# Another order of products and up blocks in the feed-forward stage of a two-layer decoder trunk

## The chip, the cores and the metric

The kernel runs on one core of a Trainium2 chip. The metric is the device time of one execution in microseconds (us): the median of several runs, on a chip that also gives one profiled execution with a trace of every engine. The engines that matter here are TensorE (PE in the rows; its weight loads are PEld), VectorE (DVE), ScalarE (ACT), GpSimd (POOL) and SyncE (SP), whose queue issues most transfers.

## The reference, cut to what matters

The program is two layers of a decoder on 256 tokens of width 2048, all in 32-bit floats. Each layer has a mixer (a projection, sliding-window attention, gated linear attention, an output projection) and a feed-forward stage. The change touches the feed-forward stage alone:

```
for l in range(2):
    ...                                          # mixer
    h = rmsnorm(x, norm2_g[l])                   # 256 x 2048
    u = jnp.square(jax.nn.relu(h @ w_up[l]))     # w_up:   2048 x 8192
    x = x + u @ w_down[l]                        # w_down: 8192 x 2048
```

## The kernel before, in words

**Exact products from two halves.** Every 512 x 512 block of a weight is loaded as f32 (1 MB), copied on ScalarE to a coarser form `wh` (L173, two instructions) and subtracted on VectorE to a rest `wl` (L174). TensorE then multiplies with both halves. A block may have its halves ready up to three blocks ahead of the one that TensorE works on, because `wh` and `wl` have three buffers (`WBUFS`): the halves of block i+3 can't be written before TensorE is done with block i. `prep` writes the halves, `fetch` issues the load. The raw weights of the up projection have two buffers.

**Up blocks.** `h @ w_up` is made 512 columns of the hidden width at a time, an index i from 0 to 15, each in four up blocks (kb 0 to 3) into four PSUM accumulators (`block_a`, L243 and L245: 16 matmuls of 512 columns and 16 of 256). After the last of the four, `up_done` moves the accumulators out (ScalarE L861, VectorE L862), and ScalarE applies relu and square (L863, L864). There are only four accumulators, so the next i waits for them.

**Chunks and products.** The hidden width is worked off in chunks c of 1024: chunk c is made of the up indices 2c and 2c+1. Its product with w_down is done for two column halves p = 0 and 1, in each with seven block products in place of eight (the Strassen-Winograd scheme), named 1, 2, 6, 5, 7, 3, 4 in the order in which they run. Each product is twelve matmuls of 512 columns (`block_p`, L257, L259, L261), after which VectorE adds the result to x (`add_to`, L892 or L894). The eighth chunk is done in the plain way, with 8 down blocks.

**The weight combinations.** A `Super` holds the four 512 x 512 quarters x, w, y, z of w_down for one chunk and half, each with one buffer. Product 1 uses x, 2 uses w. For product 6, VectorE makes x+y in place (L87) and t = that + z (L89). Two accumulating transfers on GpSimd's queue then make y+z in place (L92, for product 7) and t+w (L95, for product 4). Product 5 uses the new x, product 3 uses z. The loads of x and w are issued one block ahead of product 1's turn to be fetched, those of y and z at product 2's.

**The activation combinations.** `split` makes the two halves of a combination of the hidden activations (ScalarE L869, VectorE L870). `split_rest(c)` runs when the last up block of chunk c is done and makes six of the seven (12, s2, s1, s3, s4, 22, with four more VectorE operations, L879 to L885). Each has one buffer.

**Order.** `FFN_ORDER` starts with eight up blocks (i = 0 and 1). Then follow seven periods, one for each chunk c = 0 to 6: the 14 products of chunk c with the 8 up blocks of chunk c+1 put between them as the tuple `BETWEEN` says (0 is an up block). Written with U for an up block and the half as an index, a period before is

1a U 2a 6a U 5a 7a U 3a 4a U 1b 2b U 6b 5b U 7b 3b U 4b U

so that the last up block of chunk c+1 stands directly ahead of product 1 of chunk c+1. The instruction streams of the engines are fixed before the run by a planner, which takes the written order as priority and its own estimates of times, and so lets instructions of neighbouring blocks swap places. Each engine then goes through its stream in that order.

Of the kernel before, what the change touches and what calls it, by code (L numbers as in the profile page):

```python
# [17 lines left out]
P = 128  # L18
S = 256
NT = S // P  # L20
# [24 lines left out]
WBUFS = 3  # L45


BETWEEN = (1, 0, 2, 6, 0, 5, 7, 0, 3, 4, 0, 1, 2, 0, 6, 5, 0, 7, 3, 0, 4, 0)


@with_exitstack
def trunk(ctx, tc, x, norm1_g, w_in, q_norm_g, k_norm_g, attn_sinks, gla_gate_w,
# [9 lines left out]
    def bank(name):  # L62
        return misc.tile([P, 512], F32, tag="m", name=name)


    blocks, supers, forms = [], [], {}
    ff = [None]

    class Super:
# [14 lines left out]
        def form(self, prod):  # L84
            t = self.t
            if prod == 6:
                nc.vector.tensor_tensor(t["x"], t["x"], t["y"], ALU.add)  # L87
                t["t"] = ff[0].tile([P, 4, 512], F32, tag="qt", name=f"qt{self.name}")
                nc.vector.tensor_tensor(t["t"], t["x"], t["z"], ALU.add)  # L89
            if prod == 5:  # L90
                for a in range(0, 4, 2):
                    nc.gpsimd.dma_start(t["y"][:, a:a + 2], t["z"][:, a:a + 2],  # L92
                                        accum_op=ALU.add, max_dma_last_dim=2048)
                for a in range(0, 4, 2):
                    nc.gpsimd.dma_start(t["t"][:, a:a + 2], t["w"][:, a:a + 2],  # L95
                                        accum_op=ALU.add, max_dma_last_dim=2048)
            return t[{1: "x", 2: "w", 6: "t", 5: "x", 7: "y", 3: "z", 4: "t"}[prod]]

    def plan(layer):
        for cols in IN_CHUNKS:  # L100
            for kb in range(4):
                blocks.append((w_in[layer], kb * 512, cols))
        for n, kb in OUT_ORDER:
            blocks.append((w_out[layer], kb * 512, (n * 512, n * 512 + 512)))
        for u in FFN_ORDER:
            if u[0] == "up":
                _, i, kb = u
                blocks.append((w_up[layer], kb * 512, (i * 512, i * 512 + 512)))
            elif u[0] == "down":
                _, c, n, kb = u  # L110
                blocks.append((w_down[layer], c * 1024 + kb * 512, (n * 512, n * 512 + 512)))
            else:
                _, c, p, prod = u
                if prod == 1:
                    blocks.append(Super(w_down[layer], c * 1024, p * 1024, f"{layer}{c}{p}"))
                    supers.append((len(blocks) - 1, blocks[-1]))
                else:
                    blocks.append(supers[-1][1])
                forms[len(blocks) - 1] = prod

    IN_CHUNKS = [(1024, 1536), (0, 512), (512, 1024), (4360, 4624), (1536, 2048),
# [5 lines left out]
    FFN_ORDER = [("up", i, kb) for i in range(2) for kb in range(4)]  # L127
    for c in range(7):
        ups = [("up", i, kb) for i in (2 * c + 2, 2 * c + 3) for kb in range(4)]
        for k, step in enumerate(BETWEEN):  # L130
            if step == 0:
                FFN_ORDER.append(ups.pop(0))
            else:
                FFN_ORDER.append(("product", c, BETWEEN[:k].count(1) - (step != 1), step))
    FFN_ORDER += [("down", 7, n, kb) for n in range(4) for kb in range(2)]
    for l in range(DEPTH):
        plan(l)
# [97 lines left out]
    def block_a(accs, rhs, first, last, kts):  # L235

        i = next_block()
        wh, wl = halves.pop(i)
        for f in range(4):
            for k in range(4):  # L240
                a = rhs[kts[k]]
                fs = slice(f * P, (f + 1) * P)
                nc.tensor.matmul(accs[f], wh[:, k, fs], a,  # L243
                                 start=(first and k == 0), stop=False)
                nc.tensor.matmul(accs[f][:, :S], wl[:, k, fs], a[:, :S], start=False,  # L245
                                 stop=(last and k == 3))
            if f % 2:
                tick()
        prep_to(i + 1 + WBUFS)
# [600 lines left out]
    def feed_forward(l, norm2):  # L850
        fp = ff[0]
        hT2 = norm2.hT
        nxt = Norm(f"i{l + 1}", n1cols, (l + 1) * KT, False) if l + 1 < DEPTH else None
        ur, a = {}, {}

        def up_done(i, accs):

# [9 lines left out]
        def split(name, c, src):  # L867
            d = fp.tile([P, 4, 2, P], F32R, tag="as1" if name == "21" else f"a{name}", name=f"a{name}{l}{c}")
            nc.scalar.activation(d[:, :, 0], src, AF.Copy)  # L869
            nc.vector.tensor_tensor(d[:, :, 1], src, d[:, :, 0].bitcast(F32), ALU.subtract)  # L870
            a[name] = d

        def split_rest(c):

            a11, a21 = (ur[2 * c][:, :, T * P:(T + 1) * P] for T in range(NT))
            a12, a22 = (ur[2 * c + 1][:, :, T * P:(T + 1) * P] for T in range(NT))
            split("12", c, a12)
            s1 = fp.tile([P, 4, P], F32, tag="s1", name=f"s1{l}{c}")
            nc.vector.tensor_tensor(s1, a21, a22, ALU.subtract)  # L879
            nc.vector.tensor_tensor(a21, a11, a21, ALU.subtract)  # L880
            nc.vector.tensor_tensor(a11, s1, a11, ALU.subtract)
            split("s2", c, a11)
            split("s1", c, s1)
            split("s3", c, a21)
            nc.vector.tensor_tensor(a12, a11, a12, ALU.add)  # L885
            split("s4", c, a12)
            split("22", c, a22)

        def add_to(n, T, ps, sign=ALU.add):
            x, r = xs[T, n], norm2.r[:, T:T + 1]  # L890
# [6 lines left out]
        ps = {}  # L897
        for step in FFN_ORDER:
            if step[0] == "up":
                _, i, kb = step  # L900
                if kb == 0:
                    accs = [acc.tile([P, 512], F32, tag="a", name=f"up{l}{i}{f}")
                            for f in range(4)]
                block_a(accs, hT2, kb == 0, kb == 3, range(4 * kb, 4 * kb + 4))
                if kb == 3:
                    up_done(i, accs)
                    if nr is None:
                        nr = sm.tile([P, NT], F32, tag="nr", name=f"nr{l}")
                        nc.vector.tensor_scalar(nr, norm2.r, -1.0, None, ALU.mult)
                    if i == 0:  # L910
                        split("11", 0, ur[0][:, :, :P])
                    elif i == 15:
                        for j, k in enumerate("12"):
                            for T in range(NT):
                                split(f"{T + 1}{k}", 7,
                                      ur[14 + j][:, :, T * P:(T + 1) * P])
                    elif i % 2:
                        split_rest(i // 2)
            elif step[0] == "product":
                _, c, p, prod = step  # L920
                n1, n2 = 2 * p, 2 * p + 1
                if prod in (1, 2, 5):
                    ps[prod] = bank(f"dn{l}{c}{p}{prod}")
                o = ps[{1: 1, 6: 1, 7: 1, 4: 1, 2: 2, 5: 5, 3: 5}[prod]]
                block_p(o, a[{1: "11", 2: "12", 6: "s2", 5: "s1", 7: "s3", 3: "s4",
                              4: "22"}[prod]], prod in (1, 2, 5), True)
                if p == 1 and prod == 1 and c < 6:
                    split("11", c + 1, ur[2 * c + 2][:, :, :P])
                if prod == 1 or prod == 2:
                    add_to(n1, 0, o)  # L930
                elif prod == 6:
                    add_to(n2, 0, o, ALU.subtract)
                elif prod == 5:
                    add_to(n2, 1, o)
                elif prod == 7:
                    add_to(n2, 1, o, ALU.subtract)
                elif prod == 3:
                    add_to(n2, 0, o)
                else:
                    add_to(n1, 1, o)  # L940
            else:
                _, c, n, kb = step
                if kb == 0:
                    accs = [acc.tile([P, 512], F32, tag="a", name=f"dn{l}{c}{n}{T}")
                            for T in range(NT)]
                block_b(accs, [a["11"], a["21"]] if kb == 0 else [a["12"], a["22"]],
                        kb == 0, kb == 1, None)
                if kb == 0:
                    continue
                for T in range(NT):  # L950
                    add_to(n, T, accs[T])
                    if nxt is None:
                        nc.scalar.dma_start(
                            out[0, T * P:(T + 1) * P, n * 512:(n + 1) * 512], xs[T, n])
                if nxt is not None:
                    add(nxt.chunk(n), now[0] + 2)
# [49 lines left out]
```

## Time and profile before

| | us |
|---|---|
| median of 3 runs | 2107.3 (2105.09 to 2109.97) |
| the profiled execution | 2106.07 |
| its span, first to last instruction | 2104.1 |
| PE busy | 2039.3 (97%) |
| DVE busy | 1598.7 (76%) |
| ACT busy | 1225.6 (58%) |

The busy time of PE counts matmuls whose ends are modelled and which overlap, so a share of 97% still leaves room. What a matmul really takes is read from the distance between the starts of two that follow each other. The feed-forward stage of layer 0 lies between 368 and 1052 us. Its seven periods begin near 393 us, and they are some 89 us long.

### The profile page before, as it was taken

How to read it: one execution, taken by the hardware profiler on the slowest of the kernel's cores; microseconds unless marked ns; L12 is line 12 of the kernel's file. 1: busy time of each engine (PE TensorE's matmuls, PEld its weight loads, DVE VectorE, ACT ScalarE, POOL GpSimd, SP SyncE). 2: the span in 40 equal slices, each digit the busy share in tenths (PEclk: the TensorE clock that was granted, in tenths of full speed). 3: DMA queues.
4: the chain of work that ended last, by engine and by line, in shares of the span. 5: the costliest groups of instructions: out<-in, count | busy, mean ns of one | idle time of the engine just before them, and what ended most of it. 6: DMA issues, size and time to landing. Idle time of an engine off the chain costs nothing.

```text
span 2104.1 us, 26079 instructions
## 1 busy us (share of the span) xinstructions
PE 2039.3 (97%) x10238; PEld 1693.9 (81%) x10238; DVE 1598.7 (76%) x1442; ACT 1225.6 (58%) x1681; POOL 190.6 (9%) x198
## 2 busy tenths in 40 slices
PE   8999999999999999999999999999999999999999
PEld 7877888887777878778888878888877878778787
DVE  5676565888888888879656756658888888888884
ACT  5575554656665565656555755546665656666663
POOL 3200000001110001101002000000111001110000
PEclk9999999999999999999999999999999999999999
DMA  6544366787888878796555444578879787888864
GB/s 223 181 161 161 122 197 231 225 259 209 240 221 254 255 229 233 215 253 183 199 180 162 160 148 150 186 246 238 232 222 246 222 263 229 216 240 225 260 179 160
DMA packets 227707, 442.61 MB, mean 210 GB/s; under 512 B 8276, under 2 KB 16544, under 8 KB 227584
## 3 DMA queue, kind: packets, MB, share of 16 engines
q1 hardware_dynamic: 195472, 379.87, 52.3%
q0 software_dynamic: 30912, 58.97, 17.7%
q10 hardware_dynamic: 1200, 2.11, 0.3%
q8 instruction: 80, 1.31, 0.3%
q14 instruction: 43, 0.35, 0.0%
HBM read 380.10 MB, written 2.10 MB: 182 GB/s over the span
## 4 chain that ended last, share of the span: by engine, by line
PE 68%; DVE 14%; issue 8%; ACT 7%; DMA 3%; SPq 0%; ACTq 0%; DVEq 0%
PE up L243 14%; DVE wl L174 7%; PE up L245 7%; PE in L228 6%; PE in L227 6%; PE in L229 6%; ACT wh L173 5%; PE dn L259 4%; PE dn L261 4%; PE dn L257 4%; PE wo L228 3%; DVE qt L89 3%; PE wo L229 3%; PE wo L227 3%; DVE qx L87 2%
## 5 line engine op out<-in xcount | busy, mean ns | idle before, releaser
L174 DVE TENSOR_TENSOR wl<-raw,wh 128x2048 fp32r<-128x2048 f32 (+1 forms) x256 | 569.8, 2226 | 318.7 <-ACT wh L173 314.4
L243 PE MATMUL up<-hf,wh 128*128 128x512 f32 x2048 | 713.6, 398 | 23.7 <-ACT wh L173 12.3
L173 ACT ACTIVATE wh<-raw 128x1024 fp32r<-128x1024 f32 (+1 forms) x512 | 500.6, 1025 | 400.5 <-PE up L243 140.8
L245 PE MATMUL up<-hf,wl 128*128 128x256 f32 x2048 | 531.8, 282 | 4.2 <-DVE wl L174 4.2
L243 PEld LDWEIGHTS up<-hf,wh 128*128 128x128 f32 x2048 | 384.5, 189 | 106.3 <-ACT wh L173 16.2
L245 PEld LDWEIGHTS up<-hf,wl 128*128 128x128 f32 x2048 | 388.8, 190 | 29.2 <-DVE wl L174 10.5
L227 PE MATMUL in<-wh,hi 128*128 128x512 f32 (+1 forms) x640 | 237.9, 375 | 3.2 <-ACT hi L352 3.2
L228 PE MATMUL in<-wl,hi 128*128 128x512 f32 (+1 forms) x640 | 237.6, 373 | 0.0
L229 PE MATMUL in<-wh,hi 128*128 128x512 f32 (+1 forms) x640 | 235.1, 370 | 0.0
L257 PE MATMUL dn<-wh,as 128*128 128x512 f32 x448 | 174.1, 394 | 16.2 <-ACT as L869 16.2
L259 PE MATMUL dn<-wl,as 128*128 128x512 f32 x448 | 176.4, 394 | 3.6 <-DVE wl L174 3.4
L261 PE MATMUL dn<-wh,as 128*128 128x512 f32 x448 | 174.7, 390 | 0.0
L174 DVE TENSOR_TENSOR wl<-qx,wh 128x2048 fp32r<-128x2048 f32 x56 | 128.0, 2286 | 46.9 <-ACT wh L173 46.9
L173 ACT ACTIVATE wh<-qx 128x1024 fp32r<-128x1024 f32 x112 | 112.3, 1050 | 75.5 <-PE dn L261 39.7
L173 ACT ACTIVATE wh<-qt 128x1024 fp32r<-128x1024 f32 x112 | 112.5, 1053 | 71.3 <-DVE qt L89 36.4
L92 POOL DMA_DIRECT2D qy<-qz x56 | 68.1, 1448 | 898.5 <-DVE qx L87 821.4
L892 DVE SCALAR_TENSOR_TENSOR x<-dn,vf,x 128x512 f32<-128x512 f32 x156 | 116.0, 744 | 34.0 <-PE dn L261 19.1
L227 PEld LDWEIGHTS in<-wh,hi 128*128 128x128 f32 x640 | 120.1, 188 | 25.1 <-ACT hi L352 3.5
L228 PEld LDWEIGHTS in<-wl,hi 128*128 128x128 f32 x640 | 120.6, 188 | 22.1 <-issue 1.5
L229 PEld LDWEIGHTS in<-wh,hi 128*128 128x128 f32 x640 | 120.2, 188 | 20.1 <-issue 0.8
L257 PE MATMUL dn<-wh,a 128*128 128x512 f32 x336 | 132.5, 394 | 3.3 <-ACT a L869 3.3
L261 PE MATMUL dn<-wh,a 128*128 128x512 f32 x336 | 131.3, 391 | 0.6 <-DVE a L870 0.6
(202 smaller groups left out, 2957.7 us busy)
## 6 DMA issues: line engine op xcount, KB each, us to landing
raw<-in_w_up_dram SPq DMA_DIRECT2D x128, 1024.0 KB, 6.8
raw<-in_w_in_dram SPq DMA_DIRECT2D x63, 1024.0 KB, 5.1
raw<-in_w_out_dram SPq DMA_DIRECT2D x32, 1024.0 KB, 5.0
qx<-in_w_down_dram SPq DMA_DIRECT2D x28, 1024.0 KB, 8.4
qw<-in_w_down_dram SPq DMA_DIRECT2D x28, 1024.0 KB, 5.2
qy<-in_w_down_dram SPq DMA_DIRECT2D x28, 1024.0 KB, 9.3
qz<-in_w_down_dram SPq DMA_DIRECT2D x28, 1024.0 KB, 10.0
qy<-qz POOLq DMA_DIRECT2D x56, 512.0 KB, 6.6
```

Of the source, the lines that this page charges most:

```text
L92: nc.gpsimd.dma_start(t["y"][:, a:a + 2], t["z"][:, a:a + 2], accum_op=ALU.add, max_dma_last_dim=2048)
L173: nc.scalar.activation(wh[:, ks, :n], src[:, ks], AF.Copy)
L174: nc.vector.tensor_tensor(wl[:, :, :n], src, wh[:, :, :n].bitcast(F32), ALU.subtract)
L227: nc.tensor.matmul(o, ah, wh[:, k, :n], start=(first and k == 0), stop=False)
L228: nc.tensor.matmul(o, ah, wl[:, k, :n], start=False, stop=False)
L229: nc.tensor.matmul(o, al, wh[:, k, :n], start=False, stop=(last and k == 3))
L243: nc.tensor.matmul(accs[f], wh[:, k, fs], a, start=(first and k == 0), stop=False)
L245: nc.tensor.matmul(accs[f][:, :S], wl[:, k, fs], a[:, :S], start=False, stop=(last and k == 3))
L257: nc.tensor.matmul(o, ah, wh[:, k], start=(first and k == 0), stop=False, skip_group_check=not first)
L259: nc.tensor.matmul(o, ah, wl[:, k], start=False, stop=False, skip_group_check=not first)
L261: nc.tensor.matmul(o, al, wh[:, k], start=False, stop=(last and k == 3), skip_group_check=not first)
L892: nc.vector.scalar_tensor_tensor(x, ps, r, x, ALU.mult, ALU.add)
```

## The change

`BETWEEN` has the same 14 products and 8 up blocks in another order. A number of 10 or more is half b, one of 20 or more belongs to the next chunk. With a dash for the next chunk, the period is now

U U 2a U U 6a 5a U 7a 3a U 4a 1b U 2b 6b 5b U 7b 3b 1a' 4b

and product 1a of chunk 0 is put ahead of the first period. In the last period 1a' falls away. So the last up block of a chunk is followed by four products, three of which belong to the old chunk and one is the next chunk's first, and two up blocks stand ahead of product 2.

Three things follow in the code. The combinations s3, s4 and 22 of the next chunk can't be written while products 7b, 3b and 4b of the old one still read theirs, so `split_rest` leaves them in `late`, and each is made right after its product (in chunk 0 at once). The combinations of the eighth chunk are made after the last product in place of after the last up block. And a `Super` is looked up by its chunk and half, since two are alive at once. Apart from that, the accumulating transfer y+z is issued with product 6 and no longer with product 5.

```diff
-BETWEEN = (1, 0, 2, 6, 0, 5, 7, 0, 3, 4, 0, 1, 2, 0, 6, 5, 0, 7, 3, 0, 4, 0)
+BETWEEN = (0, 0, 2, 0, 0, 6, 5, 0, 7, 3, 0, 4, 11, 0, 12, 16, 15, 0, 17, 13, 21, 14)
...
-            if prod == 5:
                 for a in range(0, 4, 2):
                     nc.gpsimd.dma_start(t["y"][:, a:a + 2], t["z"][:, a:a + 2],
                                         accum_op=ALU.add, max_dma_last_dim=2048)
+            if prod == 5:
...
                 if prod == 1:
-                    blocks.append(Super(w_down[layer], c * 1024, p * 1024, f"{layer}{c}{p}"))
-                    supers.append((len(blocks) - 1, blocks[-1]))
-                else:
-                    blocks.append(supers[-1][1])
+                    supers[layer, c, p] = Super(w_down[layer], c * 1024, p * 1024,
+                                                f"{layer}{c}{p}")
+                blocks.append(supers[layer, c, p])
...
-        for k, step in enumerate(BETWEEN):
+        if c == 0:
+            FFN_ORDER.append(("product", 0, 0, 1))
+        for step in BETWEEN:
             if step == 0:
                 FFN_ORDER.append(ups.pop(0))
-            else:
-                FFN_ORDER.append(("product", c, BETWEEN[:k].count(1) - (step != 1), step))
+            elif step < 20 or c < 6:
+                FFN_ORDER.append(("product", c + step // 20, step // 10 % 2, step % 10))
...
             split("s1", c, s1)
-            split("s3", c, a21)
             nc.vector.tensor_tensor(a12, a11, a12, ALU.add)
-            split("s4", c, a12)
-            split("22", c, a22)
+            late[7], late[3], late[4] = ("s3", c, a21), ("s4", c, a12), ("22", c, a22)
...
-                    elif i == 15:
-                        for j, k in enumerate("12"):
-                            for T in range(NT):
-                                split(f"{T + 1}{k}", 7,
-                                      ur[14 + j][:, :, T * P:(T + 1) * P])
-                    elif i % 2:
+                    elif i % 2 and i < 15:
                         split_rest(i // 2)
+                        if i == 1:
+                            for prod in (7, 3, 4):
+                                split(*late.pop(prod))
...
+                if p == 1 and prod in late:
+                    split(*late.pop(prod))
+                if (c, p, prod) == (6, 1, 4):
+                    for j, k in enumerate("12"):
+                        for T in range(NT):
+                            split(f"{T + 1}{k}", 7, ur[14 + j][:, :, T * P:(T + 1) * P])
```

## Rows read from the trace of the kernel before

**Rows 1.** Window of one whole period: length, busy time of each engine, PEclk, DMA share, GB/s.

```profile
573.00:661.80 88.80, 84.77 (x424) 70.48 (x424) 76.78 (x61) 54.53 (x63) 9.64 (x8) 1.00 0.83 237
```

**Rows 2.** Timeline of PE, an undisturbed up block and product: start us, us, instruction.

```profile
641.62 1.07 PE L243 MATMUL up<-hf,wh 128*128 128x512 f32 x4
...
647.24 0.40 PE L257 MATMUL dn<-wh,a 128*128 128x512 f32 x1
...
649.99 0.84 PE L243 MATMUL up<-hf,wh 128*128 128x512 f32 x3
```

**Rows 3.** Timeline of PE where two chunks meet; in brackets idle time and releaser.

```profile
566.88 0.40 PE L257 MATMUL dn<-wh,a 128*128 128x512 f32 x1
...
572.32 0.28 PE L245 MATMUL up<-hf,wl 128*128 128x256 f32 x1
573.54 0.47 PE L243 MATMUL up<-hf,wh 128*128 128x512 f32 x1 [0.94 <-DVE ur L862]
...
576.27 0.28 PE L245 MATMUL up<-hf,wl 128*128 128x256 f32 x1
577.58 1.20 PE L243 MATMUL up<-hf,wh 128*128 128x512 f32 x4 [1.03 <-ACT wh L173]
579.05 0.50 PE L257 MATMUL dn<-wh,a 128*128 128x512 f32 x1 [0.27 <-ACT a L869]
...
581.13 0.50 PE L257 MATMUL dn<-wh,as 128*128 128x512 f32 x1 [1.35 <-ACT as L869]
```

**Rows 4.** Waits of PE over the whole span: us in total, times, longest us.

```profile
PE dn L257 <- ACT as L869: 16.2, 12, 1.4
PE up L245 <- DVE wl L174: 4.2, 14, 0.3
```

**Rows 5.** Timeline of DVE at the same meeting of two chunks.

```profile
570.78 2.28 DVE L174 TENSOR_TENSOR wl<-qw,wh 128x2048 fp32r<-128x2048 f32 x1
572.98 0.41 DVE L862 TENSOR_TENSOR ur<-up,us 128x256 f32<-128x256 f32 x1
573.31 0.74 DVE L892 SCALAR_TENSOR_TENSOR x<-dn,vf,x 128x512 f32<-128x512 f32 x1
...
574.30 2.28 DVE L174 TENSOR_TENSOR wl<-qt,wh 128x2048 fp32r<-128x2048 f32 x1
576.60 0.69 DVE L879 TENSOR_TENSOR s<-ur,ur 128x512 f32<-128x512 f32 x1
...
580.86 1.28 DVE L870 TENSOR_TENSOR a<-ur,a 128x512 fp32r<-128x512 f32 x2
```

**Rows 6.** Timeline of ACT: a copy that waited for TensorE, one that waited for a load.

```profile
562.11 2.01 ACT L173 ACTIVATE wh<-raw 128x1024 fp32r<-128x1024 f32 x2 [1.50 <-DMA raw<-in_w_up_dram]
...
647.33 2.01 ACT L173 ACTIVATE wh<-qx 128x1024 fp32r<-128x1024 f32 x2 [3.49 <-PE up L243]
```

**Rows 7.** Timeline of PE, the end of a product 1b.

```profile
616.19 0.39 PE L257 MATMUL dn<-wh,a 128*128 128x512 f32 x1
```

**Rows 8.** Timeline of POOL, the transfers t+w of the same half.

```profile
623.59 2.41 POOL L95 DMA_DIRECT2D qt<-qw  x2 [8.14 <-DVE wl L174]
```

**Rows 9.** Timeline of SP's queue, the reload of that half's tiles.

```profile
626.17 0.37 SPq L80 DMA_DIRECT2D qx<-in_w_down_dram  x1
633.40 0.37 SPq L80 DMA_DIRECT2D qw<-in_w_down_dram  x1
```

**Rows 10.** DMA issues over the whole span: KB each, median us to landing.

```profile
raw<-in_w_up_dram SPq DMA_DIRECT2D x128, 1024.0 KB, 6.8
...
qz<-in_w_down_dram SPq DMA_DIRECT2D x28, 1024.0 KB, 10.0
```

**Rows 11.** Window with the densest transfers, columns as in the first group.

```profile
639.00:650.00 11.00, 11.00 (x58) 9.33 (x57) 7.93 (x6) 6.04 (x6) 0.00 (x0) 1.00 1.05 386
```

**Rows 12.** Longest wait of POOL's queue over the whole span.

```profile
POOL qy L92 <- DVE qx L87: 821.4, 26, 35.6
```

**Rows 13.** Timeline of PE at the first down block of layer 0.

```profile
1013.69 0.50 PE L227 MATMUL dn<-wh,a 128*128 128x512 f32 x1 [0.35 <-DVE ur L862]
```

More of the change, by code (lines that the diff above doesn't have):

```diff
@@ L63, in bank @@
         return misc.tile([P, 512], F32, tag="m", name=name)
-    blocks, supers, forms = [], [], {}
+    blocks, supers, forms = [], {}, {}
     ff = [None]
@@ L853, in feed_forward @@
         nxt = Norm(f"i{l + 1}", n1cols, (l + 1) * KT, False) if l + 1 < DEPTH else None
-        ur, a = {}, {}
+        ur, a, late = {}, {}, {}
         def up_done(i, accs):
@@ L922, in feed_forward @@
                 if prod in (1, 2, 5):
-                    ps[prod] = bank(f"dn{l}{c}{p}{prod}")
-                o = ps[{1: 1, 6: 1, 7: 1, 4: 1, 2: 2, 5: 5, 3: 5}[prod]]
+                    ps[c, p, prod] = bank(f"dn{l}{c}{p}{prod}")
+                o = ps[c, p, {1: 1, 6: 1, 7: 1, 4: 1, 2: 2, 5: 5, 3: 5}[prod]]
                 block_p(o, a[{1: "11", 2: "12", 6: "s2", 5: "s1", 7: "s3", 3: "s4",
```

## The prediction

> **What bounds the kernel now.** I read the window of one period of the feed-forward stage first. It is 88.8 us long; PE counts as busy for 84.8, DVE for 76.8, ACT for 54.5, and the DMA engines for 83% [rows 1]. There the reader is to see that TensorE is close to full, but not full, with VectorE next. How much is missing is read from undisturbed blocks: an up block takes 647.24 - 641.62 = 5.62 us, a product 649.99 - 647.24 = 2.75 us [rows 2]. Eight up blocks and 14 products make 8 x 5.62 + 14 x 2.75 = 83.5 us. So TensorE loses 88.8 - 83.5 = 5.3 us in a period, 14 x 5.3 = 74 us in the program. The granted clock was full in that window, so there is no more in it than these waits.
>
> Next comes PE's timeline where two chunks meet. From the distances of starts, less 0.12 us for a short matmul and 0.23 for a long one (2.75 / 12; 5.62 / 16 - 0.23), four waits stand in 15 us [rows 3]:
> - 572.32 to 573.54: 1.10 us, for VectorE to empty an accumulator;
> - 576.27 to 577.58: 1.19 us, for ScalarE's `wh`;
> - 577.58 to 579.05, four matmuls: 0.55 us, for the combination 12 of product 2a;
> - 579.05 to 581.13, two matmuls: 1.62 us, for s2 of product 6a.
>
> Together 4.46 us. The list of PE's waits shows the wait for `as` 12 times and never longer than 1.4 us, one for each of the 6 meetings in a layer, so the same happens at every meeting. That is 12 x 4.46 = 53.5 us. The other 0.9 us of a period are waits for `wl` in the blocks after the two formations of x+y and t; such a wait stands in the list 14 times at `up` alone [rows 4].
>
> Why they come: DVE runs there without a pause. It makes `wl` of 2a, empties accumulators, adds, makes `wl` of 6a and only then the combinations [rows 5]. Combination 12 is used 579.05 - 566.88 = 12.2 us after the last up block, s2 after 14.3. The written order gives them 2.75 + 5.62 = 8.4 and 11.1 us.
>
> **The change, part by part.** No block, matmul or VectorE operation is added or removed; all terms are waits.
>
> *The meeting.* After the last up block now come four products, 4 x 2.75 = 11.0 us, then two up blocks, then 2a. The next up block needs its accumulators after 11.0 us; the third was emptied at 573.4, 6.5 us after the last up block's end, the fourth behind one more addition, some 1.1 later. Combination 12 is needed after 11.0 + 2 x 5.62 = 22.2 us, and took 12.2. s2 is needed after 22.2 + 2.75 + 11.2 = 36.2, and took 14.3. Three of the four waits thus lose their cause with 4 us or more to spare. The wait for `wh` came from ScalarE having relu, square and a copy in one line; that can return in another place, and I price it as new.
>
> *The run of four products*, which is what is late next. Halves of block i+3 can start when block i is done: `wh` 2.0 us [rows 6], `wl` 2.2 (start to start, 570.78 to 572.98), and two products are 5.5 us, so 1.3 us are spare. Per product DVE also has an addition, 0.7, and in three of the four a late split, 0.6 [rows 5]: 3.5 us against 2.75. It falls back 3 x 0.75 + 0.15 = 2.4 us. Less the spare 1.3, and the 0.9 us that four `wh` matmuls can run ahead of `wl` [rows 2], 0.2 us of wait remain. From above: all 4.7 us of `split_rest`'s other work (four operations of 0.7, three splits of 0.64) fall among these four too. I take 0.8 a meeting, towards the 1.19 that a misplaced `wh` costs now: 12 x 0.8 = 9.6 us. Both ends stay in the range.
>
> *Formations.* Ahead of 6a now stand two up blocks more, so its wait goes: half of 0.9, 14 x 0.44 = 6 us. 6b is still two blocks (an up block and 2b) behind 1b, and its wait stays. If 6a's stays too, the sum is 6 worse.
>
> *Start and end of the stage.* Chunk 0 makes all its combinations at once, but 2a follows 14.0 us later instead of 8.4; nothing. The eighth chunk's four splits are written after the last product; the first down block waits 0.35 us now, 0.5 with its restart [rows 13]. If the planner leaves them there it waits a copy and a subtraction, 1.25; if it pulls them up, 0. I take 0.5 more per layer, 1 us; bounds -1 and +4 (all eight pieces).
>
> *y+z with product 6.* GpSimd's queue stood idle 821 us in 26 waits for x+y itself [rows 12]. It already issues as soon as x+y is there, whichever product it is written with: 0, on both sides.
>
> *Loads.* Each load keeps its place beside its block, but on SP's queue the x and w of the next 1a are now followed at once by two up loads. That is a rival below.
>
> Sum, against the profiled execution: 2106.1 - 53.5 + 9.6 - 6 + 1 = 2057; its span is 2104.1, the rest lies around it. The median of the runs is 1.2 above it, so 2058 us.
>
> **Rivals.**
>
> *The loads come late.* The reload of w waits for the transfer t+w: it was issued 633.40 - 616.19 = 17.2 us after product 1b had ended [rows 7, 9], 9.8 after the transfer's issue [rows 8]. In the new order 30.5 us lie between 1b's end and the period's first up block (5.62 + 8.25 + 5.62 + 11.0), whose load stands behind w. The densest window moved 386 GB/s [rows 11], 2.7 us for one load. So that load lands near 17.2 + 0.5 + 2.7 + 6.8 [rows 10] = 27.2, its halves are ready at 31.4, and 30.5 to 31.4 is when they are used: on the edge. With the 10.0 us that z needs it would be 3.2 later, some 2 us of wait beyond my 0.8: 12 x 2 = 24, 2082 us. For it: ScalarE already waits for up loads, 1.5 us in one case [rows 6]. Against: before product 1a' SP has little else to do.
>
> The Trainium skill ("DMA: Bandwidth & Descriptors", Specifications) gives a core about 358 GB/s from HBM. The window's 386 is above it; by the page a load would take 2.9 us and the estimate would move by 0.4 us, against the change.
>
> *VectorE in strict written order: slower.* If the stream has `split_rest` ahead of the halves of 4b, then from the last up block's end: halves of 1a' 4.2, accumulators 0.7, relu and square 2.1 (as two copies of the same size), `split_rest` 4.7, `wl` of 4b 2.2: 13.9 us. It is needed after 3 x 2.75 + 0.23 = 8.5. Every meeting then waits 5.4 in place of 4.46: 2106.1 + 12 x 0.95 - 6 + 1 = 2113. It decides once `wl` of 4b is ready over 13.4 us after that up block. For it: the accumulators at 572.98 stood behind `wl` of 2a. Against: `wl` of 6a ran at 574.30, ahead of `s` at 576.60, though it is written after it [rows 5].
>
> The Trainium skill ("TensorE: Matmul & The Clock Gate", Architectural detail) calls the queues of ScalarE and VectorE strict first-in, first-out. By that rule what the planner wrote can't be mended by the engine, and this rival stands or falls with the stream; the trace agrees in so far as DVE worked through its list while TensorE waited 1.10 us for 0.4 us of work.
>
> *Nothing: VectorE is the bound.* It is busy for 76.8 us of a period and idle for 12.0 now; my 2058 asks that it idle about 8. If its waits for `wh` (ScalarE idles up to 3.5 us for a buffer [rows 6]) are only moved, the period stays 88.8: 2103 to 2110.
>
> **How the numbers follow.** The forecast, 2042 to 2072, has 0.53. Nearly no new wait, under 2042 (all 74 us would be 2032): 0.09. Late loads or orders like it, 2072 to 2102: 0.20. Nothing: 0.05. The slower rival: 0.13. A difference of 0.2%, 4 us, can be told from none. So faster 0.82, the same 0.05, slower 0.13. The range 2036 to 2095 leaves out the last two and a little at both ends.
>
> **What would show it.** Right: periods of 84 to 85.5 us; no wait of PE for `as`, `a` or `ur` at the meetings; the wait for `wl` ahead of 6a gone, that of 6b still there; PE's waits at 3b, 1a', 4b and the first up block under 1.5 us in sum; GpSimd's wait for x+y as long as now. Wrong: ACT idle for an up load over 2 us at each meeting (loads), PE waiting over 4 us for `wl` at 4b (written order), or DVE idling 12 us in a period of 88.

## The result and the profile after

| | before, us | after, us |
|---|---|---|
| median | 2106.72 (2105.09 to 2109.97) | 2070.51 (2068.42 to 2071.34, 4 runs) |
| the profiled execution | 2106.07 | 2071.34 |
| its span | 2104.1 | 2069.6 |

The ratio is 0.9825, 95% interval 0.9808 to 0.9842: 36.2 us faster, where 49 were forecast. In the changed kernel lines shift by two: `wh` is L175, `wl` L176, the up block L245 and L247, the product L259 to L263, x+y L88, t L90, y+z L92.

First the page after: the busy time of each engine, and the engines' shares of the chain that ended last (the chain of work followed back from the last instruction).

```profile
PE 2028.8 (98%) x10238; PEld 1699.8 (82%) x10238; DVE 1598.6 (77%) x1442; ACT 1222.4 (59%) x1681; POOL 190.5 (9%) x198
...
PE 78%; DMA 11%; DVE 6%; issue 4%; ACT 1%; SPq 0%; POOL 0%; DVEq 0%; ACTq 0%; POOLq 0%
```

The same row of the chain before:

```profile
PE 68%; DVE 14%; issue 8%; ACT 7%; DMA 3%; SPq 0%; ACTq 0%; DVEq 0%
```

The work is the same and DVE is no busier; VectorE and ScalarE have left most of the chain, and transfers have a larger share of it, 11% in place of 3%. Now TensorE's waits over the whole span (us in all, times, longest), of which [rows 4] has the old ones.

```profile
PE up L247 <- DVE wl L176: 15.3, 15, 3.8
...
PE dn L261 <- DVE wl L176: 0.2, 1, 0.2
```

No line for `as`, `a` or `ur` is left. TensorE's line for `wl` in an up block has grown from 4.2 to 15.3, and there is a second new wait, for `wh` in a product. It stands as the idle time of this group of the page:

```profile
L259 PE MATMUL dn<-wh,a 128*128 128x512 f32 x336 | 132.5, 394 | 15.0 <-ACT wh L175 15.0
```

Both stand at one place, where two chunks meet. TensorE's timeline there, with idle time and releaser in brackets:

```profile
477.91 0.49 PE L259 MATMUL dn<-wh,a 128*128 128x512 f32 x1 [1.15 <-ACT wh L175]
480.03 0.58 PE L247 MATMUL up<-hf,wl 128*128 128x256 f32 x1 [1.63 <-DVE wl L176]
```

The row at 477.91 is a single matmul of product 2a; the next row is the rest of the first up block, of which four `wh` matmuls ran before. So the planner put one matmul of 2a into that up block. Its `wh` can only be written when 4b has given its buffer back (ScalarE's copy starts at 476.80, released by 4b), so it always waits, by the distance of starts 1.30 to 1.71 us at the twelve meetings. Behind it the up block waits for its own `wl`, 0.63 to 4.09 us. Together the twelve meetings lose 34.0 us, 2.83 each. VectorE just there shows why `wl` is late:

```profile
474.83 2.29 DVE L88 TENSOR_TENSOR qx<-qx,qy 128x2048 f32<-128x2048 f32 x1 [1.43 <-DMA qy<-in_w_down_dram]
477.04 0.74 DVE L892 SCALAR_TENSOR_TENSOR x<-dn,vf,x 128x512 f32<-128x512 f32 x1
477.70 2.28 DVE L176 TENSOR_TENSOR wl<-raw,wh 128x2048 fp32r<-128x2048 f32 x1
479.90 0.69 DVE L881 TENSOR_TENSOR s<-ur,ur 128x512 f32<-128x512 f32 x1
480.50 2.28 DVE L90 TENSOR_TENSOR qt<-qx,qz 128x2048 f32<-128x2048 f32 x1
482.70 2.29 DVE L176 TENSOR_TENSOR wl<-raw,wh 128x2048 fp32r<-128x2048 f32 x1
```

The first row is x+y for product 6a, which comes only after four more up blocks and product 2a: the planner pulled it ahead of the `wl` that TensorE waits for (third row), and it stands there waiting for the load of y. t (fifth row) stands ahead of the second up block's `wl` in the same way. VectorE has this order at all twelve meetings. The worst meeting is the first of layer 1, VectorE and then TensorE:

```profile
1505.56 2.29 DVE L88 TENSOR_TENSOR qx<-qx,qy 128x2048 f32<-128x2048 f32 x1 [3.92 <-DMA qy<-in_w_down_dram]
1507.77 0.74 DVE L892 SCALAR_TENSOR_TENSOR x<-dn,vf,x 128x512 f32<-128x512 f32 x1
1508.43 2.28 DVE L176 TENSOR_TENSOR wl<-raw,wh 128x2048 fp32r<-128x2048 f32 x1
```

```profile
1510.77 0.58 PE L247 MATMUL up<-hf,wl 128*128 128x256 f32 x1 [3.83 <-DVE wl L176]
```

x+y waited for y's load, and the 4.09 us that TensorE then waited for `wl` is the longest wait of the stage. VectorE waits so at ten of the twelve meetings (columns as in TensorE's waits):

```profile
DVE qx L88 <- DMA qy<-in_w_down_dram: 9.8, 10, 3.9
```

Summed over both feed-forward stages from the distances of TensorE's starts (less the 0.12 and 0.23 us of the matmul before), time lost is 77.0 us before and 47.6 after; the rounding of these two distances makes some 4 us of each sum, which the difference does not hold. Of this the meetings are 53.5 and 34.0; stretches at half the clock (last section) about 3 and 10; all else 20 and 4. The first mixer is 3.3 us shorter too; its code is the same, and no run isolates why. The whole is 34.7 on the profiled executions.

### The profile page after: what moved, and what is told of

Same layout as the page of the kernel before. It is cut to its first block, busy times and chain, and to the rows that moved or that the text cites. A ratio compares the mean times of both kernels' runs of the same rounds, so it can differ in the third digit from the quotient of the medians.

```text
span 2069.6 us, 26124 instructions
## 1 busy us (share of the span) xinstructions
PE 2028.8 (98%) x10238; PEld 1699.8 (82%) x10238; DVE 1598.6 (77%) x1442; ACT 1222.4 (59%) x1681; POOL 190.5 (9%) x198
## 4 chain that ended last, share of the span: by engine, by line
PE 78%; DMA 11%; DVE 6%; issue 4%; ACT 1%; SPq 0%; POOL 0%; DVEq 0%; ACTq 0%; POOLq 0%
PE up L245 19%; PE up L247 10%; PE in L230 6%; PE in L229 6%; PE in L231 6%; DMA qy<-in_w_down_dram 5%; PE dn L263 5%; PE dn L261 5%; PE dn L259 5%; DVE wl L176 4%; PE wo L230 3%; PE wo L231 3%; PE wo L229 3%; DMA qt<-qw 3%; DMA raw<-in_w_up_dram 1%
## 5 line engine op out<-in xcount | busy, mean ns | idle before, releaser
L176 DVE TENSOR_TENSOR wl<-raw,wh 128x2048 fp32r<-128x2048 f32 (+1 forms) x256 | 569.6, 2225 | 317.7 <-ACT wh L175 308.1
L175 ACT ACTIVATE wh<-raw 128x1024 fp32r<-128x1024 f32 (+1 forms) x512 | 500.3, 1025 | 435.1 <-DMA raw<-in_w_up_dram 118.6
L245 PE MATMUL up<-hf,wh 128*128 128x512 f32 x2048 | 709.3, 399 | 0.0
L247 PE MATMUL up<-hf,wl 128*128 128x256 f32 x2048 | 530.1, 284 | 15.3 <-DVE wl L176 15.3
L245 PEld LDWEIGHTS up<-hf,wh 128*128 128x128 f32 x2048 | 385.9, 190 | 74.9
L247 PEld LDWEIGHTS up<-hf,wl 128*128 128x128 f32 x2048 | 392.1, 191 | 39.4 <-DVE wl L176 20.3
L263 PE MATMUL dn<-wh,as 128*128 128x512 f32 x448 | 174.6, 390 | 0.0
L259 PE MATMUL dn<-wh,as 128*128 128x512 f32 x448 | 172.8, 391 | 0.0
L175 ACT ACTIVATE wh<-qx 128x1024 fp32r<-128x1024 f32 x112 | 112.5, 1052 | 97.4 <-PE up L245 76.2
L176 DVE TENSOR_TENSOR wl<-qx,wh 128x2048 fp32r<-128x2048 f32 x56 | 128.2, 2289 | 36.9 <-ACT wh L175 36.8
L259 PE MATMUL dn<-wh,a 128*128 128x512 f32 x336 | 132.5, 394 | 15.0 <-ACT wh L175 15.0
L92 POOL DMA_DIRECT2D qy<-qz x56 | 68.1, 1447 | 694.6 <-DVE qx L88 353.4
L261 PE MATMUL dn<-wl,a 128*128 128x512 f32 x336 | 131.5, 391 | 0.2 <-DVE wl L176 0.2
L263 PE MATMUL dn<-wh,a 128*128 128x512 f32 x336 | 131.0, 390 | 0.0
L176 DVE TENSOR_TENSOR wl<-qt,wh 128x2048 fp32r<-128x2048 f32 x56 | 128.0, 2286 | 2.1 <-ACT wh L175 2.1
```

What stands on the lines that cost most here:

```text
L175: nc.scalar.activation(wh[:, ks, :n], src[:, ks], AF.Copy)
L176: nc.vector.tensor_tensor(wl[:, :, :n], src, wh[:, :, :n].bitcast(F32), ALU.subtract)
L245: nc.tensor.matmul(accs[f], wh[:, k, fs], a, start=(first and k == 0), stop=False)
L259: nc.tensor.matmul(o, ah, wh[:, k], start=(first and k == 0), stop=False, skip_group_check=not first)
L261: nc.tensor.matmul(o, ah, wl[:, k], start=False, stop=False, skip_group_check=not first)
L263: nc.tensor.matmul(o, al, wh[:, k], start=False, stop=(last and k == 3), skip_group_check=not first)
```

## The experiments

Each kernel had four runs; ratios are against the kernel before, run beside it on the same chip. After the trace three theories stood, and a *pin* below is an ordering edge that makes the planner put one instruction behind another on an engine's stream. A: the matmul of 2a in the up block is the price. B (B1 in the expectations): it only shows first what is really the late `wl`, because x+y stands ahead of it on VectorE. The third (B2) is loads: ScalarE and VectorE wait for transfers that come late, so nothing on VectorE's order helps.

**1. The matmul of 2a kept behind the first up block.** The whole product 2a is made to issue after the up blocks' last matmul.

```diff
+        with tc.issue_after(last_up[0].ins) if behind else nullcontext():
+            product(o, a, first, last, wh, wl)
```

> The changed kernel, but TensorE's stream is pinned so that all of product 2a stands behind the second up block of the period; the changed kernel's stream has one matmul of 2a ahead of the first up block's last 28, and it waits 1.3 to 1.7 us at each of 12 meetings for ScalarE's copy. Theory A (that matmul is the cause of the new wait): 12 x 1.4 = 17 us less, about 2053. Theory B (the rest half `wl` of the first up block is ready late, and the 1.3 us only stand ahead of a wait for it): the up block's first `wl` matmul starts when it did, the same time within 4 us, about 2070.

Measured 2072.88 (2070.58 to 2077.16), ratio 0.9848 [0.9828, 0.9869]: as the changed kernel. TensorE's waits, and the meeting near 566 us:

```profile
PE up L249 <- DVE wl L176: 33.9, 13, 4.5
```

```profile
566.92 0.39 PE L249 MATMUL up<-hf,wl 128*128 128x256 f32 x1 [2.77 <-DVE wl L176]
```

The wait for 2a's `wh` is gone, and the one for `wl` has grown by about as much (15.0 + 15.3 before this edit, 33.9 now). So A falls: the matmul only took a part of the same wait on itself.

**2. x+y later.** x+y and t of half a (`not self.c0`) are made to issue behind the `wl` of the second up block. `rests[j]` is the `wl` of block j, and i is 6a's block, so `i - 4` is the second up block and `i - 5` the first. No instruction is added.

```diff
+                with tc.issue_after(rests[i - 4].ins) if not self.c0 else nullcontext():
                     nc.vector.tensor_tensor(t["x"], t["x"], t["y"], ALU.add)
                     t["t"] = ff[0].tile([P, 4, 512], F32, tag="qt", name=f"qt{self.name}")
                     nc.vector.tensor_tensor(t["t"], t["x"], t["z"], ALU.add)
```

> The changed kernel, but on VectorE's stream the x+y and t of half a are pinned behind `wl` of the second up block; now x+y (2.2 us) runs ahead of `wl` of the first one. Theory B1 (x+y in front makes that `wl` late): `wl` comes 2.2 us sooner, the second wait of a meeting (0.6 to 4 us, mean 1.4) goes while the 1.3 us one stays: 12 x 1.2 = 14 us less, about 2056. Theory B2 (the reload of x, for which ScalarE waits 3 us, makes it late): nothing gained, 2066 to 2074.

Measured 2031.78 (2030.56 to 2033.74), ratio 0.965 [0.9636, 0.9665]: 38.7 us below the changed kernel. TensorE's largest wait, and VectorE at the meeting:

```profile
PE up L249 <- DVE wl L177: 4.2, 14, 0.6
```

```profile
556.99 2.28 DVE L177 TENSOR_TENSOR wl<-raw,wh 128x2048 fp32r<-128x2048 f32 x1
559.19 0.68 DVE L883 TENSOR_TENSOR s<-ur,ur 128x512 f32<-128x512 f32 x1
559.79 2.28 DVE L177 TENSOR_TENSOR wl<-raw,wh 128x2048 fp32r<-128x2048 f32 x1
561.99 2.28 DVE L89 TENSOR_TENSOR qx<-qx,qy 128x2048 f32<-128x2048 f32 x1
```

Both up blocks' `wl` now stand ahead of x+y. The time lost in both stages falls from 47.6 to 8.8 us, and the period is 83.6, the 83.5 that the prediction had for blocks without gaps. B holds, and by more than I had expected of it.

**3. Both together.**

> Both pins of e1 and e2. Theory B1: nearly the whole wait of a meeting (2.2 to 4.7 us) goes, 0.5 is left: 12 x 2.3 = 28 us less, and the half-clock stretches at the meetings with them, about 2040. Theory A: as e1, about 2053. Theory B2: as e1 by theory B, about 2070.

Measured 2032.87 (2031.81 to 2033.46), ratio 0.9654 [0.964, 0.9668]. The first pin adds nothing to the second.

**4. x+y behind the first `wl` alone.** As 2, with one `wl` less ahead of it, so that VectorE's order has x+y directly behind the `wl` that was late, not ahead of it.

```diff
-                with tc.issue_after(rests[i - 4].ins) if not self.c0 else nullcontext():
+                with tc.issue_after(rests[i - 5].ins) if not self.c0 else nullcontext():
```

> The changed kernel, with x+y and t of half a pinned behind the formation of the FIRST up block's weights instead of the second's. VectorE's order then differs from the changed kernel's only in that x+y stands right behind that one formation instead of ahead of it; the second up block's formation still stands behind x+y. Theory C (the one place ahead of the first up block's weights is the whole price): 2030 to 2036 us, as with the pin behind the second, and TensorE's waits for wl together under 6 us. Rival (the second formation, and the queue behind x+y, need the room too): 2045 us or more, with waits for wl of over 1 us each at the second up block of the pair.

Measured 2034.52 (2032.62 to 2036.0), ratio 0.9664 [0.965, 0.9678]. VectorE's timeline, TensorE's largest wait, and ScalarE's group that waits for up loads:

```profile
557.64 2.29 DVE L177 TENSOR_TENSOR wl<-raw,wh 128x2048 fp32r<-128x2048 f32 x1
559.84 2.29 DVE L89 TENSOR_TENSOR qx<-qx,qy 128x2048 f32<-128x2048 f32 x1
562.04 0.69 DVE L883 TENSOR_TENSOR s<-ur,ur 128x512 f32<-128x512 f32 x1
562.64 2.29 DVE L177 TENSOR_TENSOR wl<-raw,wh 128x2048 fp32r<-128x2048 f32 x1
...
568.31 2.29 DVE L91 TENSOR_TENSOR qt<-qx,qz 128x2048 f32<-128x2048 f32 x1
```

```profile
PE up L249 <- DVE wl L177: 5.2, 15, 0.6
```

```profile
L176 ACT ACTIVATE wh<-raw 128x1024 fp32r<-128x1024 f32 (+1 forms) x512 | 500.5, 1025 | 448.9 <-DMA raw<-in_w_up_dram 119.8
```

The move is worth 36.0 us (2070.51 - 2034.52; by the two ratios 34). The size agrees roughly: 12 x 2.2 us of x+y and 9.8 us of waiting for y make 36.2 by which that `wl` was late, and TensorE lost 34.0 at the meetings; the stretches at half the clock come on top. Two other things moved with it. The planner took 2a's first matmul out of the up block, but experiment 1 had shown that this alone is worth nothing. And t went from ahead of the second up block's `wl` to behind that of 2a (568.31), so VectorE's order differs by more than the expectation says. What t's place is worth alone no run shows; in the changed kernel TensorE waits at none of the meetings for that second `wl`. The last row settles the loads: ScalarE waits 119.8 us for up loads here and 118.6 in the changed kernel, and the 36 us are gone all the same.

**5. Which part of the change earns it: two up blocks ahead of 2a, alone.** The kernel before, with the last up block still directly ahead of 1a. The other up blocks shift by about one product, and y+z stays with product 5.

```diff
-BETWEEN = (1, 0, 2, 6, 0, 5, 7, 0, 3, 4, 0, 1, 2, 0, 6, 5, 0, 7, 3, 0, 4, 0)
+BETWEEN = (1, 0, 0, 2, 6, 5, 0, 7, 3, 0, 4, 1, 0, 2, 6, 0, 5, 7, 0, 3, 4, 0)
```

> The kernel before with one part of the change alone: two up blocks stand ahead of product 2a (1a U U 2a 6a 5a U 7a 3a U 4a 1b U 2b 6b U 5b 7b U 3b 4b U); the last up block of a chunk still comes directly ahead of 1a, and nothing else is changed. Theory D (the waits at the meeting are for what the last up block makes, and go with the distance): combination 12 is needed 14.0 us after that up block and took 12.2, s2 16.7 and took 14.3: the waits of 0.55 and 1.62 us go, those for the accumulator (1.10) and the copy (1.19) stay: 12 x 2.2 = 26 us less than before, about 2080. Theory E (VectorE's order, x+y in front, makes the waits of before too): little changes, 2098 to 2110.

Measured 2034.79 (2033.58 to 2035.43), ratio 0.9664 [0.965, 0.9679]: better than the whole change, and far better than I expected. VectorE at a meeting, and TensorE's only wait near it:

```profile
555.77 2.28 DVE L87 TENSOR_TENSOR qx<-qx,qy 128x2048 f32<-128x2048 f32 x1
557.96 2.28 DVE L174 TENSOR_TENSOR wl<-raw,wh 128x2048 fp32r<-128x2048 f32 x1
560.17 0.75 DVE L862 TENSOR_TENSOR ur<-up,us 128x256 f32<-128x256 f32 x2
...
565.89 0.75 DVE L862 TENSOR_TENSOR ur<-up,us 128x256 f32<-128x256 f32 x2
...
575.95 0.69 DVE L870 TENSOR_TENSOR as<-ur,as 128x512 fp32r<-128x512 f32 x1
```

```profile
565.37 0.39 PE L245 MATMUL up<-hf,wl 128*128 128x256 f32 x1 [0.20 <-DVE wl L174]
```

The third and fourth accumulators are emptied as late as 565.89 and no wait for `ur` comes of it: with two up blocks in a row TensorE runs other matmuls of the pair until then (the wait at 565.37 is already for the second block's `wl`). s2, which 6a needs, is ready only at 576.6 (the row at 575.95), just as 6a begins (576.20), and no wait for `a` or `as` comes of it. x+y (555.77) stands ahead of a `wl` here too, but that one is done at 560.2 and first used at 561.96. That VectorE has this time because no run of four products stands ahead is argued, not shown.

**6. The other part alone: last up block four products early, one up block ahead of 2a.**

```diff
-BETWEEN = (0, 0, 2, 0, 0, 6, 5, 0, 7, 3, 0, 4, 11, 0, 12, 16, 15, 0, 17, 13, 21, 14)
+BETWEEN = (0, 2, 0, 6, 5, 0, 7, 3, 0, 4, 11, 0, 12, 0, 16, 0, 15, 0, 17, 13, 21, 14)
```

> The changed kernel's other part alone: BETWEEN has the last up block four products earlier, but only one up block stands ahead of the next chunk's first product. Theory D (an early last up block already brings relu, square and sum of the new chunk forward, so the waits for as and a go, but x+y still stands ahead of a formation on VectorE and delays it): 2065 to 2090 us, with waits for wl of over 10 us in sum and few for as or a. Rival 1 (the early block is as good as the pair): about 2035 us. Rival 2 (one up block does not cover the new chunk's work): 2095 us or more, with waits for as, a or ur of over 1 us at each of the twelve meetings.

Measured 2069.57 (2068.08 to 2070.18), ratio 0.9829 [0.9812, 0.9845], as theory D had it in time. Its waits are small and spread, and those for `wl` come to 18.2 us, as that theory had it:

```profile
PE up L247 <- DVE wl L176: 10.5, 12, 0.9
PE dn L261 <- DVE wl L176: 7.7, 24, 0.4
PE up L245 <- ACT wh L175: 4.7, 12, 0.4
```

VectorE runs there without a pause from 554.8 to 587 us, x+y at 558.03 among it, without a wait for y.

**7. The same with x+y pinned behind its one up block's `wl`.** Is it x+y's place again, or is there no room?

> The kernel of the early last up block alone (measured at 2069.57), with x+y and t of half a pinned behind the formation of the one up block that stands ahead of product 2a. In the kernel without the pin x+y waited for no load; VectorE merely went without a pause from 554.8 to 587 us and TensorE lost some 2.9 us at each meeting in small waits for halves. Theory E (it is x+y's 2.2 us ahead of a formation that is due, load or no load): 2030 to 2045 us, TensorE's waits for wl under 8 us in sum. Rival (VectorE is simply crowded when only one up block stands between the run of four products and 2a, in whatever order): 2060 us or more, the waits standing at 2a and 6a instead.

Measured 2083.96 (2083.35 to 2084.54), ratio 0.9891 [0.9874, 0.9907]: slower by 14 than experiment 6, so theory E falls. The rival had the time, but not the place of the waits.

```profile
PE up L247 <- ACT wh L176: 22.9, 12, 1.9
```

```profile
572.07 2.29 DVE L91 TENSOR_TENSOR qt<-qx,qz 128x2048 f32<-128x2048 f32 x1
```

```profile
574.46 2.01 ACT L176 ACTIVATE wh<-qt 128x1024 fp32r<-128x1024 f32 x2 [7.16 <-DVE qt L91]
```

ScalarE stands 7.2 us behind t, which the planner put later along with x+y (572.07, in experiment 6 566.55), and the copies behind that one are late for the next up block. TensorE's waits as a whole are no fewer than in experiment 6 (28.9 us in the stages' lines, there 22.9); by the distances of TensorE's starts the larger part of the 14 us is half clock behind these waits: the mean clock over the span is 0.990, in experiment 6 0.999. With only one up block between, x+y is in the way early and is missing later. Experiment 2, which has a second up block there, could move it at no price.

**8. x+y later in the kernel before.** The pin of experiment 2 on the old order, behind the `wl` of 2a (`rests[i - 1]`).

> The kernel before with the pin of e2 alone: x+y and t of half a stand behind `wl` of product 2a on VectorE; before, they stand ahead of the last accumulators. The order of blocks is the old one. Theory D: only the accumulator's wait (1.10 us) can go, and 6a gets its halves 2 to 4 us later, when it waits anyway: 2092 to 2110. Theory E: three of the four waits go, about 2065.

Measured 2129.26 (2124.35 to 2134.53), ratio 1.0114 [1.0092, 1.0136]: slower, and above what either theory had. The pin is no gain by itself; TensorE waits:

```profile
PE up L247 <- DVE wl L175: 21.7, 28, 1.5
PE dn L259 <- ACT a L871: 16.5, 14, 1.2
PE dn L259 <- ACT as L871: 10.6, 9, 1.2
```

By the distances of TensorE's starts some 10 us of the 23 are added waits, and the larger part is stretches at half the clock: its mean over the span is 0.989 here, 0.996 in the kernel before. Both theories left the clock out.

**9. The next chunk's first product as the last of the run** (`14, 21` in place of `21, 14`), in the changed kernel and with the pin of experiment 2.

> Part of the change undone: product 1a of the next chunk stands behind the old chunk's last product 4b again (14, 21 in place of 21, 14); the up blocks stay where they are. Theory B2 (the reload of x comes late for 1a): 1a is needed one product, 2.75 us, later, ScalarE's wait of 3 us for x goes, VectorE gets through the run of four without its 2.9 us of idle time: 12 x 2.3 = 28 us less, about 2043. Theory B1: x+y still runs ahead of the up block's `wl`; a gain of 12 x 0 to 1 us, 2058 to 2070.

> e2 with product 1a of the next chunk behind 4b again (14, 21). With x+y out of the way the place of 1a should be worth little: ScalarE's wait for the reload of x (2.8 us in e2) goes, but e2 has almost no wait of TensorE left for it to end. About 2032, within 5 us of e2. If the place of 1a is itself part of the gain, 2040 or more.

Measured 2058.22 (2053.89 to 2063.08), ratio 0.9776 [0.9755, 0.9796], and 2031.47 (2030.79 to 2033.65), ratio 0.9651 [0.9637, 0.9665]. The place is worth 12 us as long as x+y is in the way, nothing once it isn't.

**10. y+z back at product 5** in the changed kernel.

> The changed kernel with the transfer y+z issued with product 5 again. GpSimd's queue waits for x+y itself: the same as the changed kernel, 2066 to 2075. If the earlier place matters, slower by 5 us or more.

Measured 2067.96 (2065.64 to 2074.86), ratio 0.9819 [0.9803, 0.9835], the same as the changed kernel within the spread.

The best versions, experiment 2 and the pinned one of 9 (2031.8 and 2031.5), beat both kernels.

## Why the prediction was right, and which term was mis-sized

The measured 2070.51 lies 1.5 us inside the range, and that is in part luck: one term was too small by 24.4 us and the clock took some 7 more, while gains that I had not counted gave about 15 back (the sum is below). Of the signs that I named, two came true: no wait for `as`, `a` or `ur`, and none for `wl` ahead of 6a. Four did not: the periods are 86.8 us on average, not 84 to 85.5; 6b's wait is gone; the meeting loses 2.83 us, not under 1.5; and GpSimd's wait for x+y changed.

**The meeting, 53.5 us off: right.** None of TensorE's waits for `ur`, `a` and `as` of [rows 3, 4] is left, as the 4 us to spare said. But it was more than was needed: experiment 5 shows that two up blocks ahead of 2a suffice, without the run of four products, which my count had as 8.4 + 5.62 = 14.0 us for a combination that took 12.2, and never priced by itself.

**The run of four products, 9.6 us: mis-sized, 34.0 measured.** This is the term that failed. I had VectorE fall back 2.4 us by its additions, late splits and halves, and took 0.8 a meeting. The count left out x+y, 2.2 us, because it belongs to 6a, behind four up blocks and 2a. The planner, free to let blocks swap, put it ahead of the first up block's `wl`, where in ten cases it first waited for a load. The sign that this could happen was there: `wl` of 6a ran at 574.30 ahead of `s` [rows 5], out of the written order; I used that row against a rival, and not as a warning that anything of 6a may come forward. The bound from above, 4.7 us a meeting, held for eleven of them (1.9 to 3.7 us); the first of layer 1 lost 5.68. Experiments 2 and 4 show the cause: with x+y, and t with it, moved behind, these waits go.

**Formations, 6 us: right in kind, half of the size.** 6a's wait for `wl` is gone as forecast, and 6b's is gone too, which I had kept. What did away with it no run isolates; it goes with experiment 5's order as well, whose largest line for `wl` is 3.4 us over the span.

**Start and end, +1: nothing.** No wait stands at the first down blocks. **y+z, 0: right** by experiment 10. But my sign for it, that GpSimd's queue would wait for x+y as long as before, fails: its idle time ahead of y+z falls from 898.5 to 694.6 us, and the part for x+y itself from 821.4 to 353.4. Before and after:

```profile
L92 POOL DMA_DIRECT2D qy<-qz x56 | 68.1, 1448 | 898.5 <-DVE qx L87 821.4 <-ACT us L861 38.8 <-DMA raw<-in_w_up_dram 38.3
L92 POOL DMA_DIRECT2D qy<-qz x56 | 68.1, 1447 | 694.6 <-DVE qx L88 353.4 <-DVE x L892 154.8 <-ACT wh L175 148.6
```

It isn't the product that y+z is written with, for in experiment 10 the same three waits are 355.6, 154.9 and 148.5 us; x+y comes earlier in the period, as VectorE's rows show.

**The sum on the profiled executions**: forecast 2057, measured 2071.3. The run of four adds 24.4, the half clock some 7; 6b takes 6.6 off, the stage's end 1, the mixer 3.3, and small waits 4. That leaves 2 us that I can't place, and the small terms were read from two traces, not isolated by runs.

**The rivals.** *Loads late* had one thing right: a load does come late at the meetings, but it is y's, through VectorE, and the up loads that I feared cost 1.8 us in all. The sign that I gave for them was a bad one: ScalarE does stand idle for an up load at every meeting, 6.4 to 9.0 us, at the third up block (its waits for up loads are 118.6 us over the span, 40.0 before), and TensorE waits there at three of the twelve meetings only, 0.4 to 0.8 us. In that rival's sum the other price of a load moves the estimate by 0.2 us (2.9 less 2.7), not by 0.4. *VectorE in strict written order* had the right mechanism: TensorE waits for a `wl` because of what stands ahead of it in a fixed stream. But it named the wrong instruction (`split_rest`; it was x+y) and so the wrong place and a price of 5.4 where 2.83 came. At 1505.56 x+y had waited 3.92 us for y, and the up block's `wl`, next but one behind it, went only at 1508.43, though ScalarE had written its `wh` by 1501.1. The Trainium skill ("TensorE: Matmul & The Clock Gate", Architectural detail) calls VectorE's queue strict first-in, first-out; the trace agrees, by that row.

*Nothing* is refuted by the gain, and VectorE could do more still: it is busy for 79.8 us of 87.0 in this window of experiment 2 (columns as in [rows 1]), and TensorE there loses 0.6:

```profile
566.00:653.00 87.00, 86.47 (x445) 73.41 (x444) 79.81 (x63) 55.09 (x65) 10.87 (x10) 1.00 0.89 250
```

**What stays open**: why the planner ranks x+y ahead of the first up block's `wl` in the new order, since its estimates were not taken apart; and how the gain of experiments 2 and 4 divides between the places of x+y and of t.

## What to carry to other kernels

Where a planner sets each engine's stream, a move of blocks moves also what belongs to none of the places counted: list every instruction that is ready early, and price it at the head of the queue of the engine that is already behind. A wait that moves to another operand when its first place is mended (experiment 1) was never that place's own; look up the engine whose operand is last and read what stands ahead of it. And try each part of a change alone: here the two up blocks alone gained 71 us and the early last up block alone 35, while both together gained 36, and 74 once x+y and t were held back.

## What the runs showed of the hardware

I had not expected the clock to answer to waits this short. Right behind six of the twelve meetings of the changed kernel the granted clock is about half, the lower of its two levels, 1.2 GHz, for 3.4 us; windows as in [rows 1], before, during and after the first of them, then one more:

```profile
470.00:477.90 7.90, 6.76 (x30) 5.25 (x28) 6.47 (x6) 7.33 (x9) 0.00 (x0) 1.00 0.72 264
480.00:483.40 3.40, 3.37 (x12) 2.94 (x13) 3.40 (x3) 0.63 (x1) 0.33 (x1) 0.55 1.10 172
483.40:490.00 6.60, 6.60 (x40) 5.80 (x39) 6.60 (x7) 0.18 (x1) 0.00 (x0) 1.00 1.06 297
...
```

```profile
742.50:745.90 3.40, 3.40 (x12) 2.93 (x11) 3.40 (x3) 0.63 (x1) 0.00 (x0) 0.51 1.10 168
```

TensorE had idled 1.30 and 1.89 us ahead of the first, 1.30 and 2.42 ahead of the second. It isn't the size of the waits alone: 1.52 and 1.38 us at 828 us, 2.90 together, were followed by full clock, and 1.69 and 1.05 at 566 us, 2.74 together, by half. In the kernel before, whose meetings lose 4.46 us in four pieces, the same happened behind two of the twelve (granted 0.58 between 937 and 941 us). In experiment 6, whose waits in the stages are at most 0.9 us each, it happened nowhere in them. Each stretch costs about 3.4 x 0.48 = 1.6 us. In experiment 2, without the waits, the mean clock over the span is 1.000, in the changed kernel 0.993.
